# Half-array attention products in adjacent pairs, three 128-key spans in stick-breaking, 128-row first chunks for transposes

## The chip, the cores and the metric

The kernel runs on one core of a Trainium2 chip. The metric is the device time of one execution in microseconds; the median of three runs of the kernel before is 1002.49 us (1002.43 to 1004.4).

## What is computed

Two layers of a decoder trunk over 272 positions: 16 learned meta tokens and 256 real ones, each a row of 1024 values. Both layers normalise, project once, run three attention branches beside each other, gate and merge them, add, normalise again and run a squared-ReLU MLP four times as wide. Cut to what matters here:

```python
proj = rmsnorm(h_res) @ w_in            # 1024 -> 6560 columns, split by branch
# A, latent attention, 8 heads: q, k of 96 values (64 + 32 rotary), v of 64
out_a = softmax(mask(q @ k.T * 96**-0.5)) @ v
# B, stick-breaking, 8 heads of 64: strictly causal, no softmax
log_keep = where(mask, log_sigmoid(-z), 0)      # z = q @ k.T / 8
a = where(mask, exp(log_sigmoid(z) + suffix_sum(log_keep)), 0);  out_b = a @ v
# C, differential, 4 heads: two maps of 64 values, one v of 128
out_c = rmsnorm((softmax(s1) - lam * softmax(s2)) @ v)
merged = sum(sigmoid(gate_b) * (out_b @ w_branch_b) for the three branches)
```

In the second layer only the 256 real tokens are needed as queries; all 272 remain as keys.

## The kernel before

Everything is kept transposed, channels on the partitions and tokens along the rows. The weights come in one stream of blocks of 1024 columns (`weight_plan`, L36). ScalarE and VectorE split each block into a high and a low fp32r half (`split`, L161 to L163), and a product is three fp32r matmuls (`mm3`, L165 to L170). These big products, `gemm` at L297 and the loops behind it, take most of the time.

The attention works in plain fp32, where one call of `PE.matmul` becomes two passes in the profile. Queries and keys are cut in chunks by `CH` (L29): positions 0 to 15 (the meta tokens), 16 to 143 and 144 to 271. The attention products are small, and some use a part of the 128 x 128 array only:

- **Stick-breaking**, `sb_pair` (L687), four pairs of heads per layer. The two heads of a pair lie on partitions 0 to 63 and 64 to 127 of one tile `hs`. For each head in turn, a mask goes into a score bank by an identity product (L697), and three score products of 64 rows add to it (L700): 16, 128 and 128 keys, the smallest first. After the exponentials come the products with the values (L736), three per head, which write 64 of 128 columns of the array; the last has 16 rows only.
- **Differential attention**, `df_head` (L755), four heads per layer. Its two maps lie on the two halves of the partitions as well. For each map, `softmax_scores` (L579) makes a score product for each chunk of queries (L588) and behind each VectorE adds the mask and takes the maximum (L591). Between the two maps the generator yields.
- **Latent attention**, `mla_pair` (L632), four pairs of heads per layer. Its queries and keys are 96 rows high. They are turned by PE transposes (L644), chunk by chunk, where the first chunk has 16 rows; `df_head` does the same at L799. The exponentials are turned by `meta_T` (L614) and `keys_T` (L607), the value products are L625, L629 and L630.

The order of the work is set at two levels. In the program, the generators of two lanes (L866) move a step on behind each projection tile: latent pairs and difference heads 0 and 2 in one lane, stick-breaking pairs and difference heads 1 and 3 in the other. Behind these, 24 gate tiles (L847) go on alone. Then the framework's scheduler places the instructions on each engine, by priority in program order, as operands and buffers come free. It can so place two products next to each other that stand apart in the program, and the reverse. Scores and masks share three banks of PSUM (`ps_s`, L98), transposes and value products another three (`ps_t`, L99).

Of the kernel before, what the change touches and what calls it, by code (L numbers as in the profile page):

```python
# [28 lines left out]
CH = ((0, 16), (16, 128), (144, 128))  # L29
NSLOT = 4 * T  # L30
# [37 lines left out]
# columns of the parameter tiles  # L68
# [10 lines left out]
def hybrid_trunk_kernel(ctx: ExitStack, tc: tile.TileContext, xin, wall, pcol, prow, consts, out):  # L79
# [118 lines left out]
    class Stream:  # L198
# [9 lines left out]
        def open(self):  # L208
            """The tile and the source of the next group of blocks."""
# [45 lines left out]
    class NormIn:  # L255
        """x * g as a split pair of tiles; 1/rms in `rstd`, to be applied after a product."""
# [40 lines left out]
    def gemm(w, h, c0, m=P, bank=0):  # L297
        """psum[m, T - c0] of one tile of columns over all of DM."""
# [45 lines left out]
    def load_rows(l, eng):  # L344
        """The layer's parameters that run along the rows, on every partition."""
        pr = st_p.tile([P, 1, PR_LAM], F32, tag="pr", name="pr", bufs=1)
        eng.dma_start(pr, prow[:, l : l + 1, :PR_LAM])
        lamv = row_p.tile([P, T], F32, tag="row", name="lamv")
        eng.dma_start(lamv[:, :256], prow[:, l, PR_LAM:])
        return pr, lamv  # L350

    def layer(l, h, rows):
# [91 lines left out]
        def make_v(vT, chunks):  # L444
            """Token-major values of one tile of 128 columns, three chunks of tokens."""
# [5 lines left out]
            S.copy(vt[:, :2], pv[:, :2])  # L451
            S.copy(vt[:n, 2], pv[:n, 2])
            return vt

# [1 line left out]
        mla = {}  # L456

        def mla_prep():
# [16 lines left out]
            # shared rotary key  # L475
# [18 lines left out]
            for c, (s0, n) in enumerate(CH):  # L494
# [29 lines left out]
            for c, (s0, n) in enumerate(CH):  # L524
# [17 lines left out]
            for c, (s0, n) in enumerate(CH):  # L542
# [23 lines left out]
        def regions(kind):  # L566
            """(column in PSUM, column of the result, first key, keys, queries, first query, mask, chunk) by chunk of queries.

            Keys lie in their order, and backwards by chunks for the first head of a pair, whose keys 0..15
            end up next to those of the second."""  # L570
            if kind == "one":
                r = [(0, 0, 0, 144, 128, 16, 128, 1), (144, 144, 0, 272, 128, 144, 0, 2), (416, 416, 0, 16, 16, 0, 144, 0)]
            elif kind == "first":
                r = [(0, 544, 128, 144, 128, 16, 144, 1), (144, 0, 0, 272, 128, 144, 144, 2), (416, 832, 256, 16, 16, 0, 144, 0)]
            else:
                r = [(0, 688, 0, 144, 128, 16, 128, 1), (144, 272, 0, 272, 128, 144, 0, 2), (416, 848, 0, 16, 16, 0, 144, 0)]
            return r[: 3 if q0 == 0 else 2]

        def softmax_scores(qa, ka, qs, pm, kind):  # L579
            """Exponentials [query, key] in pm, with their row sums' reciprocals; qs: the queries' 1/rms by chunk."""  # L580
            ps = ps_s.tile([P, 512], F32, tag="s", name="ps_s")
            lo = 0 if q0 == 0 else 1
            st = st_p.tile([P, 16], F32, tag="smx", name="smx", bufs=6)
            if q0 == 0:
                V.memset(st, 1.0)
            regs = []
            for po, o, k0, nk, nq, qo, mo, c in regions(kind):
                PE.matmul(  # L588
                    ps[:nq, po : po + nk], lhsT=qa[:, qo - q0 : qo - q0 + nq], rhs=ka[:, k0 : k0 + nk], start=True, stop=True
                )  # L590
                V.tensor_tensor_reduce(  # L591
                    out=pm[:nq, o : o + nk], in0=ps[:nq, po : po + nk], in1=maskq[:nq, mo : mo + nk], scale=1.0,
                    scalar=-3e38, op0=ALU.add, op1=ALU.max, accum_out=st[:nq, c : c + 1],
                )
                regs.append((o, nk, nq, c))
            V.scalar_tensor_tensor(
                out=st[:, 4 + lo : 7], in0=st[:, lo:3], scalar=-1.0, in1=qs[:, lo:], op0=ALU.mult, op1=ALU.mult
            )
            for o, nk, nq, c in regs:
                table_act(  # L600
                    pm[:nq, o : o + nk], pm[:nq, o : o + nk], AF.Exp, scale=qs[:nq, c : c + 1], bias=st[:nq, 4 + c : 5 + c],
                    accum_out=st[:nq, 8 + c : 9 + c],
                )
            V.reciprocal(st[:, 12 + lo : 15], st[:, 8 + lo : 11])
            return st[:, 12:], regs
# [18 lines left out]
        def pv_meta(pv, v, pt, n, stop=False):  # L624
            PE.matmul(pv[:, 0:NQ], lhsT=v[:n], rhs=pt[:n, 384 : 384 + NQ], start=True, stop=stop)  # L625

        def pv_keys(pv, v1, v2, pt):
            o1, o2 = 16 - q0, 144 - q0
            PE.matmul(pv[:, o1 : o1 + 256], lhsT=v1, rhs=pt[:, 0:256], start=False, stop=False)  # L629
            PE.matmul(pv[:, o2 : o2 + 128], lhsT=v2, rhs=pt[:, 256:384], start=False, stop=True)  # L630

        def mla_pair(j):  # L632
            vall = mla["v"]
            hts = []
            for par, hd in enumerate((2 * j, 2 * j + 1)):
                ht = qk_p.tile([P, 2 * T], F32, tag="qk", name="hm")
                hts.append(ht)
                for i, (src, g, c0) in enumerate(((mla["q"], pc[:96, l, PC_QG : PC_QG + 1], q0), (mla["k"], kgs, 0))):
                    ps = ps_t.tile([P, 512], F32, tag="t", name="ps_qkT")
                    for c, (s0, n) in enumerate(CH):  # L640
# [7 lines left out]
            sums = []  # L648
            for par, ht in enumerate(hts):
                sums.append(softmax_scores(ht[:96, :T], ht[:96, T:], mla["qs"][:, :, 2 * j + par], pm, ("first", "second")[par]))  # L650
            for rc, regs in sums:
                for o, nk, nq, c in regs:
                    S.activation(pm[:nq, o : o + nk], pm[:nq, o : o + nk], AF.Copy, scale=rc[:nq, c : c + 1])
# [7 lines left out]
            pv_meta(pv, vall[0][:, P * j : P * j + P], pts[0], 32)  # L661
            for par in range(2):
                hv = slice(64 * par, 64 * par + 64)
                cols = slice(P * j + 64 * par, P * j + 64 * par + 64)
                pv_keys(pv[hv], vall[1][:, cols], vall[2][:, cols], pts[par])
# [21 lines left out]
        def sb_pair(j):  # L687
            ht, vT = sbv[j]
            vv = make_v(vT, ((0, P), (P, P), (2 * P, 16)))
            NA = T - q0  # L690
            regs = ((0, P, 0, q0, NA), (P, P, NA, P, 144), (2 * P, 16, NA + 144, 2 * P, 16))
            W = NA + 160
            zs, As = [], []
            for par in range(2):
                rows = slice(64 * par, 64 * par + 64)
                z = ps_s.tile([P, 512], F32, tag="s", name="ps_z")
                PE.matmul(z[:, :W], lhsT=identb, rhs=maskb[:, q0:], start=True, stop=False)  # L697
                for i in (2, 0, 1):
                    k0, nk, o, c0, n = regs[i]
                    PE.matmul(  # L700
                        z[:nk, o : o + n], lhsT=ht[rows, T + k0 : T + k0 + nk], rhs=ht[rows, c0 - q0 : NQ],
                        start=False, stop=i == 1,
                    )
                zs.append(z)
# [28 lines left out]
            for par in range(2):  # L733
                hv = slice(64 * par, 64 * par + 64)
                for c, (k0, nk, o, c0, n) in enumerate(regs):
                    PE.matmul(  # L736
                        pv[hv, c0 - q0 : NA], lhsT=vv[:nk, c, hv], rhs=As[par][:nk, o : o + n], start=c == 0, stop=c == 2
                    )
            oH, oL = v4(outs["b"][0]), v4(outs["b"][1])
# [15 lines left out]
        def df_head(j):  # L755
# [24 lines left out]
            for i, ((rw, lo), tab, c0) in enumerate(zip(raw, (dgq, dgk), (q0, 0))):  # L780
# [16 lines left out]
                for c in range(lo, 3):  # L797
                    s0, m = CH[c]
# [5 lines left out]
            pms = []  # L804
            for m in range(2):
# [346 lines left out]
```

## Time and profile before

| | |
|---|---|
| median of three runs | 1002.49 us |
| profiled execution, first to last instruction | 1001.3 us |
| TensorE (PE) busy | 993.0 us, 7622 matmuls |
| VectorE (DVE) busy | 656.8 us |
| ScalarE (ACT) busy | 589.5 us |
| the chain that ended last, PE's share | 97% |

The profiled execution's own time is the span of 1001.3 us; the runs lie 1.1 to 3.1 us above it. A matmul's duration in the timeline overlaps the next one's; what a stretch of PE costs is read from the starts. Several passes of one line and tile in a row are one line there, and it shows the shape of the first. PE granted its full clock in all 40 slices of the span.

### The profile page before, as it was taken

What the parts mean: (1) busy time and instruction counts of PE and PEld (TensorE: products, weight loads), DVE (VectorE), ACT (ScalarE), POOL (GpSimd) and SP (SyncE); (2) the same over time, 40 slices, a digit from 0 to 9 for tenths busy, and PEclk for the clock granted to TensorE, in tenths of its full rate; (3) what the DMA queues carried; (4) which work ended last, traced back from release to release, by engine and by line L of the source; (5) the groups of instructions that cost most, each with busy time, mean ns of one, the idle gap of its engine ahead of it and who ended that gap; (6) DMA issues with size and microseconds to landing.
All of it is one profiled execution on the core that took longest, in us unless ns stands there. A gap on an engine that the chain in (4) does not pass through costs nothing.

```text
span 1001.3 us, 18678 instructions
## 1 busy us (share of the span) xinstructions
PE 993.0 (99%) x7622; PEld 934.3 (93%) x7622; DVE 656.8 (66%) x1329; ACT 589.5 (59%) x1176; POOL 1.9 (0%) x7
## 2 busy tenths in 40 slices
PE   8999999999999999999999999999999999999998
PEld 7888888898999999999999888888899999999998
DVE  6965447687797666655558744467868877775453
ACT  6865666667945555543436666667668465554332
POOL 0000000000000000000000000000000000000000
PEclk9999999999999999999999999999999999999999
DMA  8332222332464445455544322224334555555551
GB/s 309 142 127 85 76 94 88 123 128 85 153 209 165 169 169 171 171 188 183 178 154 158 127 85 84 96 82 161 127 128 167 192 187 195 200 177 195 200 186 52
DMA packets 23957, 149.28 MB, mean 149 GB/s; under 512 B 2800, under 2 KB 4336, under 8 KB 8256
## 3 DMA queue, kind: packets, MB, share of 16 engines
q1 hardware_dynamic: 23760, 147.77, 42.2%
q8 instruction: 60, 0.98, 0.4%
q0 software_dynamic: 112, 0.33, 0.1%
q14 instruction: 25, 0.20, 0.1%
HBM read 147.04 MB, written 1.05 MB: 148 GB/s over the span
## 4 chain that ended last, share of the span: by engine, by line
PE 97%; DVE 1%; DMA 1%; ACT 1%; SPq 0%; issue 0%; DVEq 0%
PE acc L168 25%; PE acc L169 24%; PE acc L170 24%; PE ps_s L588 3%; PE pv_s L736 2%; PE ps_z L700 2%; PE accs L170 2%; PE accs L168 2%; PE accs L169 2%; PE ps_qkT L644 1%; PE ps_p L611 1%; PE ps_z L723 1%; PE acct L169 1%; PE acct L168 1%; PE acct L170 1%; PE ps_dT L799 1%
## 5 line engine op out<-in xcount | busy, mean ns | idle before, releaser
L163 DVE TENSOR_TENSOR wl<-rawt,wh 128x1024 fp32r<-128x1024 f32 (+1 forms) x273 | 327.8, 1202 | 146.9 <-ACT wh L162 146.3
L162 ACT CAST wh<-rawt 128x1024 fp32r<-128x1024 f32 (+1 forms) x273 | 280.3, 1029 | 210.1 <-PE acc L170 185.4
L168 PE MATMUL acc<-xgH,wh 128*128 128x272 f32 (+2 forms) x1280 | 373.8, 292 | 0.0
L169 PE MATMUL acc<-xgH,wl 128*128 128x272 f32 (+2 forms) x1280 | 369.2, 288 | 0.9 <-DVE wl L163 0.9
L170 PE MATMUL acc<-xgL,wh 128*128 128x272 f32 (+2 forms) x1280 | 368.2, 288 | 0.0
L168 PEld LDWEIGHTS acc<-xgH,wh 128*128 128x128 f32 (+1 forms) x1280 | 240.0, 187 | 5.6 <-issue 2.6
L169 PEld LDWEIGHTS acc<-xgH,wl 128*128 128x128 f32 (+1 forms) x1280 | 239.8, 187 | 4.2 <-DVE wl L163 1.2
L170 PEld LDWEIGHTS acc<-xgL,wh 128*128 128x128 f32 (+1 forms) x1280 | 240.0, 188 | 2.6 <-issue 1.6
L170 PE MATMUL acc<-fL,wh 128*128 128x272 f32 (+1 forms) x320 | 91.3, 285 | 0.0
L169 PE MATMUL acc<-fH,wl 128*128 128x272 f32 (+1 forms) x320 | 91.1, 285 | 0.0
L168 PE MATMUL acc<-fH,wh 128*128 128x272 f32 (+1 forms) x320 | 91.1, 285 | 0.0
L974 ACT ACTIVATE ffr<-acc 128x272 f32<-128x272 f32 (+1 forms) x60 | 23.5, 391 | 73.4 <-PE acc L170 73.4
L170 PEld LDWEIGHTS acc<-fL,wh 128*128 128x128 f32 x320 | 60.4, 189 | 0.0
L168 PEld LDWEIGHTS acc<-fH,wh 128*128 128x128 f32 x320 | 60.4, 189 | 0.0
L169 PEld LDWEIGHTS acc<-fH,wl 128*128 128x128 f32 x320 | 60.2, 188 | 0.0
L170 PE MATMUL acc<-fHL,wh 128*128 128x272 f32 (+1 forms) x192 | 54.8, 285 | 0.0
L168 PE MATMUL acc<-fHL,wh 128*128 128x272 f32 (+1 forms) x192 | 54.7, 285 | 0.0
L169 PE MATMUL acc<-fHL,wl 128*128 128x272 f32 (+1 forms) x192 | 54.7, 285 | 0.0
L976 DVE TENSOR_TENSOR ffs<-ffr 128x272 f32<-128x272 f32 (+1 forms) x64 | 27.8, 434 | 28.5 <-ACT ffr L974 28.5
L170 PEld LDWEIGHTS acc<-fHL,wh 128*128 128x128 f32 x192 | 36.2, 189 | 0.0
L168 PEld LDWEIGHTS acc<-fHL,wh 128*128 128x128 f32 x192 | 36.2, 189 | 0.0
L169 PEld LDWEIGHTS acc<-fHL,wl 128*128 128x128 f32 x192 | 36.1, 188 | 0.0
(308 smaller groups left out, 1635.6 us busy)
## 6 DMA issues: line engine op xcount, KB each, us to landing
rawt<-wall SPq DMA_DIRECT2D x122, 1024.0 KB, 4.8
rawt<-wall SPq DMA_DIRECT2D x12, 768.0 KB, 4.3
rawt<-wall SPq DMA_DIRECT2D x4, 896.0 KB, 5.1
rawt<-wall SPq DMA_DIRECT2D x6, 256.0 KB, 6.7
xT<-xin SPq DMA_DIRECT2D x4, 272.0 KB, 6.1
rawt<-wall SPq DMA_DIRECT2D x2, 512.0 KB, 6.4
out<-xT SPq DMA_DIRECT2D x8, 128.0 KB, 4.0
rawt<-wall SPq DMA_DIRECT2D x1, 640.0 KB, 4.2
```

Of the source, the lines that this page charges most:

```text
L162: S.copy(dH, src)
L163: V.tensor_tensor(out=dL, in0=src, in1=f(dH), op=ALU.subtract)
L168: PE.matmul(ps, lhsT=aH, rhs=bH, start=start, stop=False)
L169: PE.matmul(ps, lhsT=aL, rhs=bH, start=False, stop=False)
L170: PE.matmul(ps, lhsT=aH, rhs=bL, start=False, stop=stop)
L588: PE.matmul(ps[:nq, po : po + nk], lhsT=qa[:, qo - q0 : qo - q0 + nq], rhs=ka[:, k0 : k0 + nk], start=True, stop=True)
L611: PE.transpose(p1[:, P * i : P * i + P], a, ident)
L644: PE.transpose(ps[:96, o : o + n], src[c][:n, hd, :], ident[:n, :n])
L700: PE.matmul(z[:nk, o : o + n], lhsT=ht[rows, T + k0 : T + k0 + nk], rhs=ht[rows, c0 - q0 : NQ], start=False, stop=i == 1,)
L736: PE.matmul(pv[hv, c0 - q0 : NA], lhsT=vv[:nk, c, hv], rhs=As[par][:nk, o : o + n], start=c == 0, stop=c == 2)
L974: S.activation(r[:, :NQ], ps[:, :NQ], AF.Relu)
L976: V.tensor_tensor(out=s[:, :NQ], in0=r[:, :NQ], in1=r[:, :NQ], op=ALU.mult)
```

## The change

A helper ties matmuls in a chain by edges that order instructions on PE, with no semaphore. It also ties the first of a group behind the last of the group before, in whichever branch that was.

```diff
+    behind = []
+    def in_order(group):
+        chain = [*behind, *group]
+        for a, b in zip(chain, chain[1:]):
+            tc.add_manual_dep(b.ins, a.ins.name, NOSYNC, reason="group order")
+        behind[:] = group[-1:]
```

`softmax_scores` now takes both maps (or both heads) and makes all their score products before VectorE reads any; the difference heads lose the yield between the maps. Every chunk of queries is 128 rows high:

```diff
+            pss = [ps_s.tile([P, 512], F32, tag="s", name="ps_s") for _ in maps]
+            group = []
+            for r in zip(*(regions(m[4]) for m in maps)):
+                for ps, (qa, ka, *_), (po, o, k0, nk, qo, mo, c) in zip(pss, maps, r):
+                    group.append(
+                        PE.matmul(
+                            ps[:, po : po + nk], lhsT=qa[:, qo - q0 : qo - q0 + P], rhs=ka[:, k0 : k0 + nk], start=True, stop=True
+                        )
+                    )
+            in_order(group)
```

In `sb_pair` the three key spans are 0 to 127, 128 to 255 and 144 to 271 (the last one overlaps, and a mask constant leaves its own 16 keys), the two masks come first, and the products of the two heads alternate. The value products do the same:

```diff
-            vv = make_v(vT, ((0, P), (P, P), (2 * P, 16)))
+            vv = make_v(vT, ((0, P), (P, P), (144, P)))
-            regs = ((0, P, 0, q0, NA), (P, P, NA, P, 144), (2 * P, 16, NA + 144, 2 * P, 16))
+            regs = ((0, 0, q0, NA), (P, NA, P, 144), (144, NA + 144, 2 * P, 16))
...
+            for z in zs:
+                group.append(PE.matmul(z[:, :W], lhsT=identb, rhs=maskb[:, q0:], start=True, stop=False))
+            for k0, o, c0, n in regs:
+                for par, z in enumerate(zs):
...
+                            z[:, o : o + n], lhsT=ht[rows, T + k0 : T + k0 + P], rhs=ht[rows, c0 - q0 : NQ],
+                            start=False, stop=k0 == 144,
...
+            in_order(group)
...
+            for c, (k0, o, c0, n) in enumerate(regs):
+                for par in range(2):
...
+                            pv[hv, c0 - q0 : NA], lhsT=vv[:, c, hv], rhs=As[par][:, o : o + n], start=c == 0, stop=c == 2
...
+            in_order(group)
```

The value products of the other two branches go through `in_order` too, in pairs for the latent branch. With all three value chunks 128 rows high, `make_v` copies them at once on ScalarE instead of in two copies. Where queries and keys are projected, normalised and turned (`mla_prep`, `mla_pair`, `df_head`), the first chunk is positions 0 to 127 instead of 0 to 15; of its result the next chunk overwrites all but the first 16 columns. In `meta_T` the first layer's 16-row product becomes a transpose:

```diff
+CW = ((0, 128), (16, 128), (144, 128))
...
-                    for c, (s0, n) in enumerate(CH):
+                    for c, (s0, n) in enumerate(CW):
...
-                PE.matmul(p0[:n, :16], lhsT=pm[:16, a : a + n], rhs=ident[:16, :16], start=True, stop=True)
+                PE.transpose(p0[:n, :P], pm[:, a : a + n], ident)
...
-    c[:, C_MTC : C_MTC + 16] = np.where(k[:, None] >= j[None, :], f4(NEG), f4(0))
+    c[:, C_MTC : C_MTC + 16] = np.where((k[:, None] >= 112) & (k[:, None] - 112 < j[None, :]), f4(0), f4(NEG))
```

The rest of the diff removes comments.

## Rows read from the trace of the kernel before

**Rows 1.** Busy line of the page; waits of PE for other engines, the longest.

```profile
PE 993.0 (99%) x7622; PEld 934.3 (93%) x7622; DVE 656.8 (66%) x1329; ACT 589.5 (59%) x1176; POOL 1.9 (0%) x7
...
PE warm L1008 <- DVE ones L141: 1.1, 1, 1.1
```

**Rows 2.** Timeline of PE: start, us, line, operation, count; lone difference scores in both layers.

```profile
174.53 0.29 PE L169 MATMUL acc<-xgH,wl 128*128 128x272 f32 x1
174.65 0.29 PE L170 MATMUL acc<-xgL,wh 128*128 128x272 f32 x1
174.87 0.72 PE L588 MATMUL ps_s<-hd 64*128 64x272 f32 x2
175.52 0.40 PE L168 MATMUL acc<-xgH,wh 128*128 128x272 f32 x1
175.76 0.29 PE L169 MATMUL acc<-xgH,wl 128*128 128x272 f32 x1
...
669.57 0.51 PE L588 MATMUL ps_s<-hd 64*128 64x144 f32 x2
670.01 0.39 PE L168 MATMUL acc<-xgH,wh 128*128 128x256 f32 x1
```

**Rows 3.** Timeline of PE: difference scores of two maps side by side.

```profile
184.16 0.52 PE L588 MATMUL ps_s<-hd 64*128 64x144 f32 x4
184.60 0.39 PE L170 MATMUL acc<-xgL,wh 128*128 128x272 f32 x1
```

**Rows 4.** Timeline of PE: value products of the latent branch.

```profile
87.95 0.66 PE L629 MATMUL pv_m<-pt,vtok 128*64 128x256 f32 x4
88.43 0.40 PE L630 MATMUL pv_m<-pt,vtok 128*64 128x128 f32 x4
88.65 0.62 PE L736 MATMUL pv_s<-sba,vtok 128*64 128x272 f32 x2
```

**Rows 5.** Timeline of PE: stick-breaking scores, first head and the start of the second.

```profile
47.78 0.35 PE L697 MATMUL ps_z<-maskb,identb 128*128 128x432 bf16 x1
48.05 1.11 PE L700 MATMUL ps_z<-hs 64*16 64x16 f32 x6
49.10 0.36 PE L697 MATMUL ps_z<-maskb,identb 128*128 128x432 bf16 x1
```

**Rows 6.** Timeline of PE: stick-breaking value products, two heads, and the product behind.

```profile
61.42 2.19 PE L736 MATMUL pv_s<-sba,vtok 128*64 128x272 f32 x12
63.54 0.39 PE L168 MATMUL acc<-xgH,wh 128*128 128x272 f32 x1
```

**Rows 7.** Groups of PE by line and shape: passes, busy us, mean ns.

```profile
L588 PE MATMUL ps_s<-hd 64*128 64x272 f32 x32 | 9.5, 441 | 0.0
...
L736 PE MATMUL pv_s<-sba,vtok 16*64 16x16 f32 x32 | 4.5, 214 | 0.0
...
L644 PE MATMUL ps_qkT<-ct,kall 16*96 16x16 f32 x16 | 3.5, 216 | 0.0
...
L799 PE MATMUL ps_dT<-ct,draw 16*128 16x16 f32 x12 | 2.7, 228 | 0.2 <-DVE draw L795 0.2
...
L644 PE MATMUL ps_qkT<-ct,qall 16*96 16x16 f32 x8 | 1.7, 216 | 0.0
...
L588 PE MATMUL ps_s<-hm 96*16 96x16 f32 x16 | 1.7, 183 | 0.0
```

**Rows 8.** Timeline of PE: transposes of the latent branch, in threes.

```profile
92.67 0.57 PE L644 MATMUL ps_qkT<-ct,qall 16*96 16x16 f32 x3
93.17 0.57 PE L644 MATMUL ps_qkT<-ct,kall 16*96 16x16 f32 x3
```

**Rows 9.** Busy us of PE, PEld, DVE, ACT early in layer 0's attention.

```profile
30.00:60.00 30.00, 30.00 (x196) 26.14 (x195) 28.08 (x71) 24.81 (x54) 0.00 (x0) 1.00 0.38 138
```

**Rows 10.** VectorE: L835 (a head's result), L851 (gate tile): ns, first to last start.

```profile
L835 DVE SCALAR_TENSOR_TENSOR on<-pv_d,dog,rso x8: 476/488/501, 203.5 to 749.3; 128x272 f32<-128x272 f32 x4, 128x256 f32<-128x256 f32 x4
...
L851 DVE TENSOR_TENSOR gate<-acc,rstd x48: 399/425/443, 168.6 to 758.8; 128x272 f32<-128x272 f32 x24, 128x256 f32<-128x256 f32 x24
```

More of the change, by code (lines that the diff above doesn't have):

```diff
@@ L450, in make_v @@
                 PE.transpose(pv[:n, c, :], vT[:, s0 : s0 + n], ident)
-            S.copy(vt[:, :2], pv[:, :2])
-            S.copy(vt[:n, 2], pv[:n, 2])
+            if n == P:
+                S.copy(vt, pv)
+            else:
+                S.copy(vt[:, :2], pv[:, :2])
+                S.copy(vt[:n, 2], pv[:n, 2])
             return vt
@@ L575, in regions, with softmax_scores @@
             else:
-                r = [(0, 688, 0, 144, 128, 16, 128, 1), (144, 272, 0, 272, 128, 144, 0, 2), (416, 848, 0, 16, 16, 0, 144, 0)]
+                r = [(0, 688, 0, 144, 16, 128, 1), (144, 272, 0, 272, 144, 0, 2), (416, 848, 0, 16, 0, 144, 0)]
             return r[: 3 if q0 == 0 else 2]
-        def softmax_scores(qa, ka, qs, pm, kind):
-            ps = ps_s.tile([P, 512], F32, tag="s", name="ps_s")
+        def softmax_scores(maps):
             lo = 0 if q0 == 0 else 1
[L583 to L589, printed above, removed]
-                )
[L591 to L605, printed above, removed]
@@ new lines, in softmax_scores @@
+            in_order(group)
+            made = []
+            for ps, (qa, ka, qs, pm, kind) in zip(pss, maps):
+                st = st_p.tile([P, 16], F32, tag="smx", name="smx", bufs=6)
+                regs = []
+                for po, o, k0, nk, qo, mo, c in regions(kind):
+                    V.tensor_tensor_reduce(
+                        out=pm[:, o : o + nk], in0=ps[:, po : po + nk], in1=maskq[:, mo : mo + nk], scale=1.0,
+                        scalar=-3e38, op0=ALU.add, op1=ALU.max, accum_out=st[:, c : c + 1],
+                    )
+                    regs.append((o, nk, c))
+                V.scalar_tensor_tensor(
+                    out=st[:, 4 + lo : 7], in0=st[:, lo:3], scalar=-1.0, in1=qs[:, lo:], op0=ALU.mult, op1=ALU.mult
+                )
+                for o, nk, c in regs:
+                    table_act(
+                        pm[:, o : o + nk], pm[:, o : o + nk], AF.Exp, scale=qs[:, c : c + 1], bias=st[:, 4 + c : 5 + c],
+                        accum_out=st[:, 8 + c : 9 + c],
+                    )
+                V.reciprocal(st[:, 12 + lo : 15], st[:, 8 + lo : 11])
+                made.append((st[:, 12:], regs))
@@ L607, in keys_T @@
+            return made
         def keys_T(pt, parts):
@@ L624, in pv_meta, with pv_keys @@
         def pv_meta(pv, v, pt, n, stop=False):
[L625 to L630, printed above, removed]
+            return PE.matmul(pv[:, 0:NQ], lhsT=v[:n], rhs=pt[:n, 384 : 384 + NQ], start=True, stop=stop)
+        def pv_keys(pvs):
+            made = []
+            for w, (o, n) in enumerate(((16 - q0, 256), (144 - q0, 128))):
+                for pv, vs, pt in pvs:
+                    made.append(
+                        PE.matmul(
+                            pv[:, o : o + n], lhsT=vs[w], rhs=pt[:, 256 * w : 256 * w + n], start=False, stop=w == 1
+                        )
+                    )
+            return made
         def mla_pair(j):
@@ L660, in mla_pair @@
             pv = ps_t.tile([P, 512], F32, tag="t", name="pv_m")
-            pv_meta(pv, vall[0][:, P * j : P * j + P], pts[0], 32)
+            group = [pv_meta(pv, vall[0][:, P * j : P * j + P], pts[0], 32)]
+            halves = []
             for par in range(2):
@@ L664, in mla_pair @@
                 cols = slice(P * j + 64 * par, P * j + 64 * par + 64)
-                pv_keys(pv[hv], vall[1][:, cols], vall[2][:, cols], pts[par])
+                halves.append((pv[hv], (vall[1][:, cols], vall[2][:, cols]), pts[par]))
+            in_order(group + pv_keys(halves))
             oH, oL = v4(outs["a"][0]), v4(outs["a"][1])
@@ L732, in sb_pair @@
             pv = ps_t.tile([P, 512], F32, tag="t", name="pv_s")
[L733 to L737, printed above, removed]
+            group = []
+            for c, (k0, o, c0, n) in enumerate(regs):
+                for par in range(2):
+                    hv = slice(64 * par, 64 * par + 64)
+                    group.append(
+                        PE.matmul(
+                            pv[hv, c0 - q0 : NA], lhsT=vv[:, c, hv], rhs=As[par][:, o : o + n], start=c == 0, stop=c == 2
+                        )
                     )
+            in_order(group)
             oH, oL = v4(outs["b"][0]), v4(outs["b"][1])
```

67 lines of the change are left out of this document (33 added, 34 removed).

## The prediction

> **What bounds the kernel now.** I read the page's busy line and the waits of TensorE (PE) first. PE is busy for 993.0 of 1001.3 us, and the longest it ever waited for another engine is 1.1 us, at the start [rows 1]. The reader should see a PE that is never short of work: behind the start, time falls only where PE's own list of matmuls gets shorter. So I price everything in start-to-start times on PE, not in durations: a matmul's duration contains pipeline depth that the next one covers.
>
> The yardstick is a big fp32r product: 0.12 to 0.13 us from start to start (174.53 to 174.65), called 0.126 below. The half-array products stand out against it. A lone difference score of 272 keys, fp32 and so two passes, starts 0.22 after the product before it (0.09 over the yardstick), lasts 0.65 until the next big product starts, and that one takes 0.24 (0.10 over) [rows 2]. A lone one of 144 keys lasts 0.44. The 0.21 between them is 128 columns twice, so 0.83 ns per column and pass: 272 keys stream for 0.45 and 144 for 0.24, and 0.20 is left over inside each. **Changing the array's shape and back thus costs 0.09 + 0.20 + 0.10 = 0.39 us.** The 0.10 by which the first product behind a change is longer I read as its weight load, which nothing covers. A lone 272 costs 0.39 + 0.45 = 0.84, a lone 144 0.63, and a 16-key product with 16 weight columns, whose load is short, some 0.33 (an estimate: 0.39 + 0.03 - 0.09).
>
> The decisive row is a pair: four passes of 144 keys (two maps, two passes each, in the two row halves) last 0.44 (184.16 to 184.60), exactly what one map alone took [rows 3]. The two halves run at once, today, wherever they happen to stand next to each other. The column halves do too: eight passes, four of 256 and four of 128 columns, take 0.70 (87.95 to 88.65), when one half alone would stream (256 + 128) x 2 x 0.83 ns = 0.64 [rows 4].
>
> **The change part by part**, first the products that don't run in pairs now.
>
> *Stick-breaking scores.* One head takes 1.32 (47.78 to 49.10): a mask product, then six passes of 16, 272 and 144 columns; the second head starts again with a full-array mask, so the halves never meet [rows 5]. Two heads are 2.64 + 0.10 = 2.74. After: two masks in a row, 2 x 0.18 (the 0.27 from 47.78 to 48.05 less 0.09), one change of shape 0.39, pairs of 272 and 144 columns at 0.45 + 0.24, and the third span. That one now loads 128 weight columns instead of 16 for 16 moving ones. No row shows it. Its ends are 0.03 (streaming alone) and 0.23 (two uncovered loads of 0.10 and the streaming); I take 0.12, as the first load lies under the pass before it. Sum 1.56, so 1.18 less; eight such pairs (four per layer): 9.4 us.
>
> *Stick-breaking values.* Twelve passes last 2.12 (61.42 to 63.54); with 0.09 in front and 0.10 behind that is 2.31 [rows 6]. The 16-row tails force a change of shape inside each head: 32 tail passes, four per pair, so eight pairs [rows 7]. After: change 0.33 (estimated: 64 weight columns load in half the time), pairs 0.45 + 0.24, and the tail, now 128 rows, between 0.03 and 0.13, taken as 0.07: 1.09. Saving 1.22 x 8 = 9.7 us.
>
> *Difference scores.* There are 32 passes of 272 keys [rows 7], so 16 products, 16 of 144, and eight of 16 in layer 0. In the trace nine of the 272s stand alone (0.85 each), six in three pairs (0.85 to 0.97), one beside a 144 (0.95); ten 144s stand in five pairs (0.64), five alone (0.63); the eight 16s stand alone (0.33). Together 7.7 + 2.7 + 0.95 + 3.2 + 3.1 + 2.7 = 20.3 us. After: one group per head, 0.39 + 0.24 + 0.45, and 0.12 for the 16-key pair in layer 0: 1.20 x 4 + 1.08 x 4 = 9.1. Saving 11.2 us.
>
> *16-row pieces made 128 rows high.* Three transposes, the first of 16 rows, follow each other at 0.50 (92.67 to 93.17) [rows 8]. Three full ones, one pass each, stream 3 x 128 x 0.83 ns = 0.32, and without the 16-row one no shape changes; 0.33. Saving 0.17 on each of 16 + 8 triples of L644 and 12 of L799 [rows 7]: 6.1 us. L619, called in layer 0 alone by four latent pairs and four difference heads, becomes a transpose: by the same rows about 0.15 x 8 = 1.2. The latent branch's eight 16-query scores (16 passes) [rows 7] lose a change of shape (0.28 with the small load) and get two loads of 0.10: 0.08 x 8 = 0.6. Up-projections of chunk 0 stream the same columns with wider weights: nothing, as the longer load lies under the pass before it; without that cover 0.1 on each of the 18 passes.
>
> *Where it costs nothing.* VectorE and ScalarE do the same column counts on more partitions, one ScalarE copy less per stick-breaking pair, and no memsets. The latent value products are paired already [rows 4], their scores are 96 rows high and can't be. The edges add no semaphore, but tie the attention groups of both lanes into one order: a group whose score bank is late (three such banks; a stick-breaking pair holds two) holds back the groups behind it, and big products fill in. No transfer moves.
>
> The sum: 9.4 + 9.7 + 11.2 + 6.1 + 1.2 + 0.6 = 38.2 us. Two things take some back. VectorE is busy for 28.08 of 30 us at the start of layer 0's attention [rows 9], so the 2.4 us that go from one pair there, and as much in layer 1, may not be cashed; and a group whose second bank is late falls apart and pays 0.39 again. For both I take 3 us, between 0 and 12. Then 1001.3 - 38.2 + 3 = 966.1 for the span; the runs' median of 1002.49 lies 1.2 above the span, so **967.3, rounded to 967 us**.
>
> **The rivals.**
>
> *Groups fall apart (0.14).* The scheduler places a matmul when its operands and bank are there. Where the second bank comes late, the pair is separated, as the two stick-breaking heads sometimes are today. If half of the 24 paired groups lost their pairing (0.7 us each for the second head's streaming, 0.39 for the change), 13 us come back: 980. For it: three banks for two lanes. Against it: pairs that are ready together stand together today.
>
> *VectorE takes over in the attention stretches (0.08).* If what goes in the crowded stretches is not cashed (difference heads 11.2 + 2.0 and the first pairs 4.8, half of it), 9 us come back: 976. Against it: VectorE has 656.8 us of work in all [rows 1].
>
> *Passes of a pair in strict order (0.04).* If one product's two passes had to start before the other's first, each group would pay one pass, 0.23, more: 24 x 0.23 = 5.5, so 972. The pair at 184.16 speaks against it: with an extra pass it would have lasted 0.56, not 0.44 [rows 3]. The Trainium skill (TensorE: Matmul & The Clock Gate, Part 3, "The mechanism") says that matmuls start and end in strict program order; by that rule, if a product's passes are issued back to back, it would come out so, and the trace does not agree.
>
> *The halves don't run at once in the new order (0.05).* Then only changes of shape go: 0.36 + 0.39 + 2 x 0.81 = 2.37 for scores (0.37 less), 0.33 + 2 x 0.76 = 1.85 for values (0.46 less), difference heads 2.01 and 1.77 (5.2 less in all): 6.6 + 5.2 + 7.9 = 19.7 less, 983. That is also the case in which the change does not do what it says.
>
> *Slower: the one order starves PE (0.04).* The last head's result comes at 749.3 and the last gate tile at 758.8 in layer 1 [rows 10]: the lanes end 9.5 us before PE runs out of gates. With some 19 us less PE work per layer the gates end sooner. Were a lane held back by late banks so that its last result came over 9.5 us behind the new end of the gates, PE would wait. It becomes slower than before only if it waits over 19 us per layer, with lanes 28 us later against the gates than now: at 21 us, 1006. Against it: a difference head has one step less, which brings the lanes forward.
>
> **How the numbers follow.** The forecast has 0.65: 967, on its own 957 (3 us of losses gone, every unknown load covered, and some separate value products of today joined as well) to 977. The range reaches from 956 to 982: it takes in the fallen-apart groups, VectorE and strict order, and leaves out most of the last two rivals and the forecast's tails. 0.2%, 2 us, is about what can be told from no change, as the three runs lie within 2 us. Faster 0.95, same 0.01, slower 0.04: no rival but the starved one comes near the old time, and it may fall a little short of it.
>
> **What would show it.** Right: eight stretches of stick-breaking scores of about 1.6 us with both masks first, value stretches of 1.1 instead of 2.3, one stretch of 1.1 to 1.2 per difference head, transposes in threes at 0.33, no 16-row matmuls in L644, L799 and L619's place, and PE still over 98% busy. Wrong: big products between the members of a group; pairs that last twice one half; PE waiting for ScalarE or VectorE around the first pairs of a layer or ahead of the merge; a third span that costs over 0.25.

## The result, and the profile after

The changed kernel takes 977.22 us (median of four runs, 976.67 to 978.06) against 1003.44 us for four runs of the kernel before beside them: a ratio of 0.974, with a 95% interval of 0.9725 to 0.9755. That is 26.2 us less, where the prediction had some 36 less. The profiled execution has a span of 975.6 us, 25.7 less than before.

The busy line and the chain of the page of the changed kernel, to be held beside [rows 1]:

```profile
PE 964.4 (99%) x7614; PEld 926.5 (95%) x7614; DVE 654.2 (67%) x1313; ACT 588.7 (60%) x1168; POOL 1.9 (0%) x7
...
PE 91%; DVE 4%; ACT 3%; DMA 1%; issue 0%; SPq 0%; DVEq 0%
```

PE is still busy for 99% of the span, but its share of the chain that ended last has gone from 97% to 91%: VectorE and ScalarE now hold 7% of it, where they held 2%. The waits of PE for other engines say where (us in total, times, longest):

```profile
PE ps_dT L840 <- DVE draw L836: 1.4, 4, 0.8
PE acc L179 <- DVE wl L173: 1.2, 2, 0.9
PE warm L1049 <- DVE ones L142: 1.1, 1, 1.1
PE acc L178 <- DVE gate L892: 0.9, 2, 0.6
```

The first, before the transposes of a difference head, stood at 0.3 in the kernel before, and the last was not there. How busy the engines were in two stretches of the changed kernel (busy us of PE, PEld, DVE, ACT and POOL, then the granted clock, DMA share and GB/s), the first to be held beside [rows 9]:

```profile
30.00:60.00 30.00, 29.75 (x200) 27.29 (x199) 28.52 (x72) 25.41 (x53) 0.00 (x0) 1.00 0.40 141
195.00:199.00 4.00, 3.17 (x26) 2.95 (x25) 4.00 (x13) 3.53 (x8) 0.00 (x0) 1.00 0.75 262
```

Now the groups themselves, in the timeline of PE of the changed kernel. Stick-breaking scores of two heads, the answer to [rows 5]; their values [rows 6]; the scores of a difference head [rows 2, 3]; two triples of latent transposes [rows 8]:

```profile
48.40 0.53 PE L731 MATMUL ps_z<-maskb,identb 128*128 128x432 bf16 x2
48.86 1.10 PE L736 MATMUL ps_z<-hs 64*128 64x272 f32 x12
49.89 0.39 PE L178 MATMUL acc<-xgH,wh 128*128 128x272 f32 x1
50.12 0.29 PE L179 MATMUL acc<-xgH,wl 128*128 128x272 f32 x1
...
61.37 1.00 PE L775 MATMUL pv_s<-sba,vtok 128*64 128x272 f32 x12
62.30 0.39 PE L178 MATMUL acc<-xgH,wh 128*128 128x272 f32 x1
...
170.25 1.10 PE L601 MATMUL ps_s<-hd 64*128 64x144 f32 x12
171.28 0.39 PE L179 MATMUL acc<-xgH,wl 128*128 128x272 f32 x1
...
65.42 0.49 PE L672 MATMUL ps_qkT<-ct,qall 128*96 128x128 f32 x3
65.75 0.49 PE L672 MATMUL ps_qkT<-ct,kall 128*96 128x128 f32 x3
66.08 0.49 PE L672 MATMUL ps_qkT<-ct,qall 128*96 128x128 f32 x3
```

Read from start to start, with 0.09 in front of a half-array group where a big product stands there and 0.10 behind, as in the prediction: two masks and twelve passes 1.49 + 0.10 = 1.59 us (priced 1.56), values 0.93 + 0.19 = 1.12 (1.09), a difference head in layer 0 1.03 + 0.19 = 1.22 (1.20), a triple of transposes 0.33 (0.33). **Where a group runs undisturbed, its price was right within 0.03 us.**

So the missing 10 us lie elsewhere. I added up, over the whole trace, the start-to-start times of each kind of product, with what the big product in front and the one behind lasted longer than their own 0.127 (layer 0) or 0.118 us (layer 1). "Best" is the last column's kernel, the eleventh of the experiments:

| us on PE | before | after | difference | priced | best |
|---|---|---|---|---|---|
| stick-breaking scores and masks | 21.75 | 14.34 | -7.4 | -9.4 | 12.58 |
| stick-breaking values | 18.32 | 8.48 | -9.8 | -9.7 | 8.49 |
| difference scores | 19.08 | 9.73 | -9.4 | -11.2 | 10.74 |
| latent transposes | 13.69 | 11.57 | -2.1 | -4.1 | 9.57 |
| difference transposes | 7.97 | 8.39 | +0.4 | -2.0 | 7.24 |
| turned exponentials | 13.56 | 14.25 | +0.7 | -1.2 | 14.66 |
| latent scores | 14.91 | 12.92 | -2.0 | -0.6 | 12.93 |
| latent values | 12.63 | 13.72 | +1.1 | 0 | 11.37 |
| running sums in stick-breaking | 14.43 | 15.11 | +0.7 | 0 | 16.51 |
| stalls between big products | 0.24 | 1.51 | +1.3 | 0 | -0.07 |

The rows shown come to -26.5, and -38.2 was priced; all others together are +0.9. The transposes and the turned exponentials, 7.3 us of the price, brought 1.0. In the timeline one sees how. Before the transposes of a difference head, then inside the latent triples, and a stick-breaking group that fell apart:

```profile
197.83 0.29 PE L180 MATMUL acc<-xgL,wh 128*128 128x272 f32 x1
198.95 0.55 PE L840 MATMUL ps_dT<-ct,draw 128*128 128x128 f32 x3 [0.83 <-DVE draw L836]
...
113.55 0.29 PE L178 MATMUL acc<-xgH,wh 128*128 128x272 f32 x1
113.89 0.54 PE L672 MATMUL ps_qkT<-ct,kall 128*96 128x128 f32 x3
...
587.13 0.95 PE L736 MATMUL ps_z<-hs 64*128 64x256 f32 x8
588.42 0.28 PE L642 MATMUL ps_p<-ct,pmm 128*32 128x128 f32 x1 [0.35 <-ACT pmm L684]
588.55 0.49 PE L632 MATMUL ps_p<-ct,pmm 128*128 128x128 f32 x3
...
589.40 0.40 PE L736 MATMUL ps_z<-hs 64*128 64x16 f32 x4
589.73 0.39 PE L178 MATMUL acc<-xgH,wh 128*128 128x272 f32 x1
```

At 197.83 PE has a big product in hand, and the next instruction of its list is a transpose whose operand VectorE has not finished: 1.12 us pass from start to start instead of 0.13. VectorE is not idle meanwhile: from 195 to 199 it is busy for 4.00 of 4.00 us, so at this place PE waits for a full VectorE. At 113.55 the same happens in small, 0.34 instead of 0.13, and no wait is named there, since the product's modelled duration of 0.29 covers nearly all of it. At 587.13 the third spans of a pair stand behind eight transposes of exponentials, before which PE waits for ScalarE, and take 0.33 of their own. Of the eight stick-breaking score groups two (586.67 and 609.21) lost their third span in this way, one (66.40) is cut behind the first product of one head, and two have only a mask standing apart; of the eight difference groups one is split. Seven value groups are whole; of the eighth (108.03) the first product is drawn in among value products of the latent branch. Two latent value groups, which running sums cut behind their first product before, are now cut inside a pair. Why the scheduler cuts these groups is open: a third span needs no operand and no bank that the products ahead of it don't have already.

### The profile page after: what moved, and what is told of

Its sections match the earlier page's. It is cut to its first block, busy times and chain, and to the rows that moved or that the text cites. A ratio compares the mean times of both kernels' runs of the same rounds, so it can differ in the third digit from the quotient of the medians.

```text
span 975.6 us, 18642 instructions
## 1 busy us (share of the span) xinstructions
PE 964.4 (99%) x7614; PEld 926.5 (95%) x7614; DVE 654.2 (67%) x1313; ACT 588.7 (60%) x1168; POOL 1.9 (0%) x7
## 3 DMA queue, kind: packets, MB, share of 16 engines
HBM read 147.04 MB, written 1.05 MB: 152 GB/s over the span
## 4 chain that ended last, share of the span: by engine, by line
PE 91%; DVE 4%; ACT 3%; DMA 1%; issue 0%; SPq 0%; DVEq 0%
PE acc L178 24%; PE acc L180 24%; PE acc L179 24%; PE ps_s L601 2%; PE accs L180 2%; PE accs L178 2%; PE accs L179 2%; PE ps_qkT L672 1%; ACT wh L172 1%; DVE wl L173 1%; PE ps_p L632 1%; PE ps_z L760 1%; PE acct L179 1%; PE acct L178 1%; PE acct L180 1%; PE pv_m L654 1%
```

## The experiments

The theories. The prediction's own account: the edges keep the pairs together, halves of the array run at once, and each term is worth its price. **Theory W** came out of the table above: PE's order is fixed when the program is built, and a PE that gets through its products sooner comes to the transposes and turned exponentials before VectorE, ScalarE or a bank of PSUM is ready, with no other work placed in between. Its rivals: VectorE is short of capacity; the edges hold the lanes back; a piece was priced too high. Line numbers in rows are those of each kernel. Times below are medians with the kernel before on the same chip; "less" is against that kernel. The changed kernel is 26.2 less.

### One and two: without the edges, and with edges inside a group only

```diff
     def in_order(group):
-        chain = [*behind, *group]
-        for a, b in zip(chain, chain[1:]):
...
+        pass
```

> The change without its order-only edges; all else (shared score groups, overlapping span, 128-row chunks) stays. Theory A, the edges are what puts the halves side by side: 6 to 15 us slower than the change (983 to 992), with score and value groups broken up in the timeline. Theory B, writing the products alternately in the program is enough, because ready products of one step are placed together anyway: within 2 us of the change's 977.

978.6 us against 1002.95, ratio 0.9756 [0.9743, 0.977]: 24.4 less. The same three score groups are broken (the one at 586.67 at 587.50), and two more, whole but for a mask in the changed kernel, stand one head after the other with big products between. One of them:

```profile
94.21 0.35 PE L728 MATMUL ps_z<-maskb,identb 128*128 128x432 bf16 x1
94.49 1.09 PE L733 MATMUL ps_z<-hs 64*128 64x272 f32 x6
...
96.12 0.36 PE L728 MATMUL ps_z<-maskb,identb 128*128 128x432 bf16 x1
96.41 1.09 PE L733 MATMUL ps_z<-hs 64*128 64x272 f32 x6
```

By kinds the stick-breaking scores take 16.79 instead of 14.34, and the latent values 12.59 instead of 13.72. The second kernel keeps the edges inside a group and drops the one to the group before:

```diff
-        chain = [*behind, *group]
+        chain = group
```

> The change with edges inside each group, but no edge from one group to the next. If the one order over both lanes holds groups back (three stick-breaking groups stand broken up in the change's timeline): 1 to 4 us faster, 973 to 976. If that order is what keeps the lanes' groups from mixing: 1 to 4 us slower, 978 to 981.

976.44 against 1002.95, ratio 0.9735 [0.9722, 0.9748]: 26.5 less, and the groups stand as in the changed kernel. So program order alone places most pairs, and the edges inside a group keep two of the eight score groups together. They are worth some 2 us: on one chip the runs of this kernel, 976.40 to 976.77, and those without edges, 978.41 to 978.94, don't overlap, although the two ratios' intervals touch. Tying the lanes into one order costs nothing that shows. What splits the three groups is not an edge.

### Three: first chunks of 16 rows again

```diff
-CW = ((0, 128), (16, 128), (144, 128))
+CW = CH
```

> The change with 16-row first chunks for the projections and transposes again (the scores and the stick-breaking spans stay 128 high). My sum priced these pieces at 6.1 us: then 983. If PE, spared the 16-row pieces, only waits for ScalarE and VectorE in their place (theory W), about half comes back: 979 to 981, and the time PE is late at the fourth transpose of a latent pair (0.16 to 0.21 us each now) shrinks. If they never cost anything: 977.

978.92 against 1002.95, ratio 0.9761 [0.9748, 0.9774]: 24.0 less. The 128-row pieces are so worth 2.2 us in the changed kernel, and 6.1 was their price. The triple itself answers to its price (0.50, at 65.22 to 65.72, against 0.33):

```profile
65.22 0.57 PE L672 MATMUL ps_qkT<-ct,kall 16*96 16x16 f32 x3
65.72 0.57 PE L672 MATMUL ps_qkT<-ct,qall 16*96 16x16 f32 x3
```

In the sum by kinds, the latent transposes take 13.62 here and 11.57 in the changed kernel, the difference transposes 9.95 and 8.39, but the stalls between big products 0.30 and 1.51 and the stick-breaking values 8.82 and 8.48. Part of the saving is handed back at other products.

### Four: the products of a pair one head after the other

```diff
-            for r in zip(*(regions(m[4]) for m in maps)):
-                for ps, (qa, ka, *_), (po, o, k0, nk, qo, mo, c) in zip(pss, maps, r):
+            for ps, (qa, ka, *_, kind) in zip(pss, maps):
+                for po, o, k0, nk, qo, mo, c in regions(kind):
...
-            for k0, o, c0, n in regs:
-                for par, z in enumerate(zs):
+            for par, z in enumerate(zs):
+                for k0, o, c0, n in regs:
...
-            for c, (k0, o, c0, n) in enumerate(regs):
-                for par in range(2):
+            for par in range(2):
+                for c, (k0, o, c0, n) in enumerate(regs):
```

> The change with the products of a score or value group issued one head (or map) after the other, still chained by edges: same instructions, same number of changes of the array's shape, but no two halves side by side. If pairs run at once, as priced: 6.5 us more in the stick-breaking scores, 6.1 in the values, 6.0 in the difference scores, 18.6 in all: 996. If PE has waits that this hides (theory W): 10 to 15, 987 to 992. If the gain was only in the changes of shape: within 3 us of 977.

982.71 against 1002.95, ratio 0.9801 [0.9788, 0.9815]: 20.2 less, so the alternation is worth 6 us and not the 19 that were expected. The timeline of PE in this kernel, for the score and the value group of the first pair:

```profile
48.87 1.66 PE L736 MATMUL ps_z<-hs 64*128 64x272 f32 x12
50.46 0.39 PE L178 MATMUL acc<-xgH,wh 128*128 128x272 f32 x1
...
61.60 1.51 PE L775 MATMUL pv_s<-sba,vtok 128*64 128x272 f32 x12
63.04 0.39 PE L178 MATMUL acc<-xgH,wh 128*128 128x272 f32 x1
```

Twelve passes take 1.59 here and 1.03 in the changed kernel; one head alone took 1.05 [rows 5]. The second head so adds 0.54, though its columns stream for 0.45 + 0.24 + 0.03 or more. The two heads overlap even here: the first product of the second starts beside the last but one of the first. My expectation had taken one head to end before the other begins. What holds of it: the halves run at once, and alternating the products is what makes the overlap whole.

### Five and six: each half of the change alone, on the kernel before

The stick-breaking part alone (three spans of 128 keys, shared masks and alternating products in `sb_pair`, with the edges; `softmax_scores`, `df_head` and the chunks as before):

> The kernel before with the stick-breaking part of the change alone (three 128-key spans, masks first, heads alternating, edges). My sum: 9.4 for the scores and 9.7 for the values, 19.1 less than before's 1003, so 984. If PE pays in waits what it saves here (theory W): 12 to 16 less, 987 to 991. If part of the price was counted twice in the sum (theory D, changes of shape between neighbouring small groups): 1 to 2 less gain, 985 to 986, with no more waits than before.

988.56 against 1003.15, ratio 0.9853 [0.984, 0.9867]: 14.6 less. By kinds: values 9.0 less and scores 8.2 less, and 1.1 more each for turned exponentials and latent values, 0.6 for the running sums.

The shared score products alone (`softmax_scores` for both maps, with the edges, and `df_head` without the yield between the maps; the rest as before):

> The kernel before with the shared score products of the differential and the latent branch alone (both maps in one group, 128 query rows, edges, one step less per difference head). My sum: 11.2 and 0.6, so 991. Theory W: PE then waits at the difference heads' transposes and turned exponentials, 2 to 4 us come back: 993 to 995. Theory D: 9 to 10 less, 993 to 994, without new waits; the timeline tells it from W.

996.95 against 1003.15, ratio 0.9938 [0.9925, 0.995]: 6.2 less. By kinds: difference scores 9.5 less, latent scores 2.0 less, **difference transposes 3.7 more**. The waits of PE in this kernel, and its timeline before one such transpose:

```profile
PE ps_dT L819 <- DVE draw L815: 1.7, 3, 1.2
...
PE ps_dT L819 <- DVE smx L612: 1.0, 1, 1.0
```

```profile
175.81 0.29 PE L179 MATMUL acc<-xgL,wh 128*128 128x272 f32 x1
177.32 0.57 PE L819 MATMUL ps_dT<-ct,draw 16*128 16x16 f32 x3 [1.22 <-DVE draw L815]
178.11 0.39 PE L177 MATMUL acc<-xgH,wh 128*128 128x272 f32 x1 [0.22 <-DVE gate L872]
```

Here the loss is seen alone: 1.51 us from 175.81 to 177.32 instead of 0.13, at transposes that the edit did not touch. VectorE works without a gap from 172.94 until their operand is there at 177.17, and in it, from 173.68 to 175.46, are mostly the masks and maxima of both maps of the head before. The parts alone and the 128-row pieces come to 14.6 + 6.2 + 2.2 = 23.0, near the 26.2 of the whole: the shortfall belongs to the parts, not to their meeting.

### Seven and eight: one step more between a difference head's rotation and its transposes

In both kernels a difference head's rotation on VectorE and its transposes belong to one step, with no other lane's turn between them. Theory W says that PE work placed there takes the wait away, with nothing removed from any engine:

```diff
+            ropes = []
             for i, ((rw, lo), tab, c0) in enumerate(zip(raw, (dgq, dgk), (q0, 0))):
...
                 V.tensor_tensor(out=r6, in0=r6, in1=bv, op=ALU.add)
+                ropes.append((i, rw, lo, c0))
+            yield
+            for i, rw, lo, c0 in ropes:
                 ps = ps_t.tile([P, 512], F32, tag="t", name="ps_dT")
```

> The change with one more step in each difference head, between the rotary work of VectorE and the transposes of its result. Theory W, PE stands in front of these transposes because they are placed before VectorE is done (waits of 0.3 to 1.0 us there, some 2 us in all): 1.5 to 2.5 us faster than the change's 977, so 975. If these waits only move on to the next user, or the lanes get late: 977 to 979.

973.19 against 1003.15, ratio 0.97 [0.9687, 0.9713]: 30.0 less, 3.8 more than the change. The place that stood at 197.83 to 198.95:

```profile
198.84 0.29 PE L179 MATMUL acc<-xgH,wl 128*128 128x272 f32 x1
198.97 0.49 PE L844 MATMUL ps_dT<-ct,draw 128*128 128x128 f32 x3
199.21 0.37 PE L180 MATMUL acc<-xgL,wh 128*128 128x272 f32 x1
```

The transposes start at the same time as in the changed kernel, 198.97 and 198.95, but eight big products have been done on the way. By kinds the difference transposes fall from 8.39 to 6.51, the stalls from 1.51 to 0.55, and the value transposes and the sums over a head's result by 0.4 each; nothing else moves by over 0.2. That is more than the 1.5 to 2.5 us expected.

A rival is that this step is good in itself, with or without the change. The same edit on the kernel before:

> The kernel before with the step between the rotary work and the transposes of a difference head, and nothing else. Theory W: before the change PE had some 0.8 us of waits at these transposes (three of them), so at most 1 us faster than 1003: 1002 to 1003. If the step is worth 4 us by itself, whatever the change did to PE: 999.

1005.08 (eleven runs) against 1002.96 (fifteen), ratio 1.0021 [1.0012, 1.003]: 2.1 us slower. The difference transposes do not gain there: 7.86 against 7.97, with waits for the rotation of 0.5 in all against 0.3 (my expectation's 0.8 was too high). What the step does cost is seen in the timelines of this kernel and of the kernel before, one difference head each:

```profile
218.77 0.51 PE L588 MATMUL ps_s<-hd 64*128 64x144 f32 x2
219.21 0.39 PE L169 MATMUL acc<-xgH,wl 128*128 128x272 f32 x1
```

```profile
219.47 0.52 PE L588 MATMUL ps_s<-hd 64*128 64x144 f32 x4
219.92 0.39 PE L168 MATMUL acc<-xgH,wh 128*128 128x272 f32 x1
```

Two passes in 0.44 instead of four in 0.45: the maps that stood side by side by chance in the kernel before are parted, and the difference scores take 23.02 instead of 19.08. With these 3.9 us taken out, the step would have been some 1.8 faster here as well (an estimate: 3.9 less 2.1), of which the sum by kinds finds 0.8 at the sums over the heads' results and next to nothing at the transposes. So of the 3.8 us of the seventh experiment the 1.9 at the transposes and the 1.0 of stalls, neither of which this kernel had to lose, belong to the change; for the rest it is not shown.

### Nine: the meta keys' value products 128 rows high

The value products of the latent branch for the 16 meta keys still have 32 rows, those of the difference heads 16. Filled up with zeros to 128 rows (in layer 1 only for the difference heads; GpSimd clears what is added), they would change no shape:

```diff
+            G.memset(vall[0], 0.0)
...
-            meta_T(pts[0], pm, 32, (832, 672, 256))
+            meta_T(pts[0], pm, P, (832, 672, 256))
...
-            group = [pv_meta(pv, vall[0][:, P * j : P * j + P], pts[0], 32)]
+            group = [pv_meta(pv, vall[0][:, P * j : P * j + P], pts[0], P)]
```

> The change with the meta keys' value products 128 rows high (zeros below the 16 or 32 rows; the difference heads in layer 1 alone), so that no 32-row shape is left in these groups. By the price of a change of shape: 0.4 in each of four difference heads and 0.2 in each of eight latent pairs, 3.2 us: 974. Theory W: half of it comes back in waits, 975 to 976.

975.24 against 1003.15, ratio 0.9721 [0.9707, 0.9734]: 27.9 less, 1.7 more than the change, within the intervals' width. By kinds the value products of the latent branch and of the difference heads take 2.4 us less, where 3.2 was priced, and the turned exponentials, now 128 columns wide, 0.45 more. Waits at the difference transposes stay as in the changed kernel (1.4 and 0.2 us): the time is the one that theory W gave, but no new wait stands behind it.

### Ten to twelve: together, and the 128-row pieces once more

The step and the full height in one kernel:

> The change with both amendments, the step ahead of the transposes and the meta value products at full height. They act at different places, so 4.0 and 2.0 add: 971. If theory W holds for what full height saves, it is less: 972 to 973.

970.93 against 1002.96, ratio 0.9678 [0.9665, 0.9692]: 32.0 less, so the two gains add. And with a step between the transposes of the two heads of a latent pair as well, of which the fourth triple was late:

```diff
                     S.activation(ht[:96, i * T : i * T + T - c0], ps[:96, : T - c0], AF.Copy, scale=g)
-            yield
+                yield
```

> The same with one more step in each latent pair, between the transposes of its two heads: the fourth group of transposes waits 0.11 to 0.21 us for a bank in seven of eight pairs, 1.2 us in all. Theory W: 1 us faster, 970. If one step more per pair brings the lane behind the gates: 971 to 975.

**968.65 against 1002.96, ratio 0.966 [0.9647, 0.9673]: 34.3 less, the best kernel of the study**, 8.1 below the change. The latent transposes fall from 11.57 to 9.57, in which the priced 4.1 are whole; all eight stick-breaking score groups are whole too, at 12.58 in all (priced 8 x 1.56 = 12.5). Three difference groups are split here (10.74 in all against 9.73 in the change). The timeline at the triple that had been late by 0.21:

```profile
117.48 0.49 PE L675 MATMUL ps_qkT<-ct,qall 128*96 128x128 f32 x3
117.81 0.49 PE L675 MATMUL ps_qkT<-ct,kall 128*96 128x128 f32 x3
118.06 0.37 PE L178 MATMUL acc<-xgH,wh 128*128 128x272 f32 x1
```

Last, the 16-row chunks in this kernel, by the edit of the third experiment, which tells whether these pieces were priced too high or their gain was eaten by waits:

> The fastest version so far (968.65) with 16-row first chunks for projections and transposes again. In the change itself this cost 1.7 us only. Theory W, their price of 6.1 us was right and waits at the latent transposes and the difference heads' hid the rest; these waits are gone or smaller here: 3.5 to 6 us slower, 972 to 975. If the price was wrong: under 2.5 slower, below 971.

972.64 against 1002.93, ratio 0.97 [0.9687, 0.9713]: 4.0 slower than with 128 rows. The latent transposes take 13.80 instead of 9.57: 4.2, where 4.1 was priced. The difference transposes take 8.08 instead of 7.24: 0.8, where 2.0 was priced. The same edit brings 2.2 us in one kernel and 4.0 in another: for the latent transposes the price was right, and what comes of it depends on whether the next thing is ready.

## Why the prediction was right, and where it fell short

The measured 977.2 us lies in the stated range of 956 to 982, but 10 us above the forecast and just outside its own 957 to 977. The range held it because of rivals that did not happen as they were described, and in that there is luck. The prices of the groups were right, and the term for what does not arrive was not.

- **What bounds the kernel** (PE's list, read in start-to-start times): right. Everything that came off the time came off that list.
- **0.39 us per change of shape, halves that run at once**: right. Undisturbed groups came within 0.03 us of their price, and the third span, bounded by 0.03 and 0.23 and taken as 0.12, takes 0.13 a pair (a difference head's products last 1.03 with a 16-key pair in layer 0 and 0.90 without it in layer 1).
- **Difference scores, 11.2**: 9.4 came. The kernel before spent 19.1 on them by the sum over its trace and not 20.3, and one group of eight is split.
- **128-row pieces, 6.1, and L619's transpose, 1.2**: 1.0 came by kinds; the third experiment finds 2.2 for the 128-row pieces alone. The price itself held for the latent transposes in the twelfth, and for L619 where its group stands undisturbed: a latent pair's turned exponentials, with the longer product behind them, take 1.14 before (at 108.03) and 0.98 after (at 125.31). What came off there was lost again at the turned exponentials of the difference heads and of layer 1, which stand later or apart.
- **"For both I take 3 us, between 0 and 12"** is the step that failed. 38.2 - 25.7 = 12.5 us did not arrive. It named two losses: the crowded start of the attention, and groups that fall apart. The first is not there: between 30 and 60 us VectorE is busy for 28.52 us, against 28.08 [rows 9], and PE still for 29.75 of 30. The second is there for 2.0 us of stick-breaking scores, some 0.7 of the split difference group and 1.1 of the latent values. Another 1.2 is the kernel before, sized too high at the difference scores. Most of the rest is a third loss that the step did not price: waits at products that the change leaves alone or only makes higher (at the latent and difference transposes alone 4.4 us of their price did not come). PE's order is set at build time, so work taken from PE between a VectorE or ScalarE instruction and the transpose that needs it turns into a wait. It was a matter of placing: the extra step of the seventh experiment takes nothing off any engine, and gives 3.8 us.
- The prediction had named the place. "A difference head has one step less, which brings the lanes forward" stands in it as an argument against waits; the waits came all the same, at the transposes of the heads' rotations. Whether the missing step brought them, or the two maps' masks and maxima that now stand in one block in VectorE's list, is not shown: no run puts back the one without the other.
- **The rivals.** "VectorE takes over" has the time (976) and not the mechanism: VectorE has 654.2 us of work in the changed kernel and 655.0 in the best, which is 8.1 faster. At the difference heads VectorE is full for some us at a time, and that is where PE waits, but the seventh experiment takes the wait away with VectorE's work unchanged. "Groups fall apart" happened to five of 24 paired groups (three of scores, one difference head, one of values), not half. Strict order and halves that don't run at once are refuted by the 1.03 us of a difference head's twelve passes, which would have been 1.26 and more. PE is not starved: 98.9% busy.

Still open: the best kernel is 34.3 us below the kernel before, and some 2 of these belong to the full-height products, which the change doesn't have; 38.2 less 32 leaves 6 us uncashed. The turned exponentials (14.66), the running sums (16.51) and the split difference groups are where the table shows them; no run tried these. That the fourth latent triple waits for one of the three banks of `ps_t` is argued from their number and not shown.

## What to carry to other kernels

Price what is taken off a busy engine's list from undisturbed rows, start to start, and then go through what stands behind each removed piece: which operand from another engine comes next, and how long ago was it started. Where that margin was covered by the removed work, move a turn of other work into the gap in the same change; here two added `yield`s brought some 6 of the 12.5 us that were missing. And try an edit in the kernel in which it will stay, since the same 16-row pieces were worth 2.2 us in one and 4.0 in the other, and the same extra step 3.8 less in one and 2.1 more in the other.

## What the runs showed of the hardware

Two fp32 products on the two halves overlap although one head's products all stand before the other's in the program. In the fourth experiment the second head added 0.54 us instead of the 0.72 or more that its columns stream: by the starts of the passes, its first one begins 6 ns behind the first head's first 144-key pass, with that head's other 144-key pass and both its 16-key passes still to come. The Trainium skill (TensorE: Matmul & The Clock Gate, Part 3, "The mechanism") has matmuls start in strict program order. By products the trace does not agree for these two-pass ones; whether it does by passes is open, as no row shows in which order the passes were handed to PE.

In the profiled execution of that experiment PE's clock fell to half. The stretches of time (busy us of PE, PEld, DVE, ACT and POOL, then the granted clock, DMA share and GB/s), and the timeline around the fall:

```profile
207.00:212.30 5.30, 3.24 (x26) 2.41 (x23) 5.23 (x23) 3.69 (x14) 0.00 (x0) 1.00 0.02 5
212.30:219.00 6.70, 6.63 (x28) 6.22 (x29) 4.59 (x19) 2.78 (x11) 0.00 (x0) 0.50 0.84 312
219.00:226.00 7.00, 7.00 (x51) 6.38 (x51) 4.10 (x20) 6.46 (x20) 0.00 (x0) 0.99 0.00 1
```

```profile
211.25 0.52 PE L840 MATMUL ps_dT<-ct,draw 128*128 128x128 f32 x3 [1.22 <-DVE smx L616]
...
212.99 0.43 PE L178 MATMUL acc<-xgH,wh 128*128 128x272 f32 x1
213.21 0.43 PE L179 MATMUL acc<-xgH,wl 128*128 128x272 f32 x1
```

Before the fall PE had been busy for 3.24 of 5.30 us, with waits of 0.64 and 1.22 for ScalarE and VectorE; the granted clock was then 0.50 (1.2 GHz) for 6.7 us, big products came 0.22 us apart instead of 0.126, and 28 products were done where the changed kernel did 49 in the same stretch. The 21 products fewer are 2.6 us at 0.126 each (an estimate). This execution took 985.43 us and the other three, of which no trace is kept, 981.74 to 982.77. Here the waits of PE so cost more than their own length. The changed kernel kept the full clock in this stretch.
